# The second score product of prompt attention: over all 128 rows with a zero-padded low part of the query, and the odd heads' value rows kept in the tile of the norm factors

## The chip, the cores and the metric

One core of one Trainium2 chip runs the kernel. The metric is device microseconds (us) of one execution; the kernel before was timed three times (2570.28, 2571.55 and 2572.80 us, median 2571.55 us). The engines are named as in the profile: PE is the matrix engine, and PEld its weight loads, DVE the vector engine, ACT the scalar engine, POOL the general engine, and SP the queue that issues most of the DMAs.

## The reference, cut to what matters

The kernel does one inference step of a two-layer decoder trunk for a prompt of 1024 tokens and for 8 x 8 sampled tokens. The change lies in the stick-breaking attention of layer 0 over the prompt: 8 heads of 64, strictly causal, no softmax. For each head and each block of 128 queries:

```python
z = jnp.einsum('nqhd,nkhd->nhqk', qblk, k, preferred_element_type=jnp.float32) * scale + bias_f
mask = k_pos[None, :] < pblk[:, None]
log_1m = jnp.where(mask, jax.nn.log_sigmoid(-z), 0.0)
after = lax.cumsum(log_1m, axis=3, reverse=True) - log_1m
logw = jnp.where(mask, jax.nn.log_sigmoid(z) + after, -jnp.inf)
wgt = jnp.exp(logw)
return jnp.einsum('nqhk,nkhd->nqhd', wgt.astype(v.dtype), v)
```

## The kernel before

All large products are made from operands split in two: a high part, rounded to the matrix engine's reduced float32 format, and the low part that is left (the line L235, `mm3`, makes three matmuls of each product in this way). PE is fed by one stream of matmuls in program order. The prompt is worked on in two halves of the tokens: group A holds the tokens 0 to 511, group B the rest with the 64 sampled tokens. The attention isn't a stage of its own. It is a generator, and the loops of the large products (the input projection of group B, the output projection and the channel mixer of group A) call it at fixed places: each call puts a piece of attention between two stretches of L235 matmuls. So the order of the work on each engine is fixed by the program; nothing is moved at run time. In the profile the attention of group A runs from about 228 to 335 us beside the input projection of B, and that of group B from about 344 to 565 us beside the output projection and the channel mixer of A.

The function `attention` handles 32 units in each group: 8 heads, and for each of them four blocks of 128 queries, the longest key range first (512, 384, 256 and 128 keys in A; 1024, 896, 768 and 640 in B).

- `operands` (L951 to L963) prepares a head. Two heads share a 128-partition tile, the even one in the partitions 0 to 63, the odd one in 64 to 127. Call the head's own half r and the other one o. The tile `kt` holds the high part of the keys in r (ACT) and the low part in o (DVE); `qa` holds the high part of the queries in both halves (ACT). `qz` is one tile for all heads: its half r gets the low part of the queries (DVE, L963).
- `s1` (L971 to L988) makes the scores. One matmul over 128 rows takes `qa` and `kt`, so both the high and the low part of the keys with the high part of the queries; a second one over 64 rows takes the half r of `qz` and of `kt`, and adds the low part of the queries. Both are on L981. Ranges over 512 keys are cut in two column blocks, so group B has four such matmuls in a unit and group A has two (of at least 256 columns). ACT makes two sigmoids out of the scores (L986), POOL sets one column (L988).
- `s2`, one unit later, is on DVE: two scans (L995, L998) and one product (L1000) that makes the weights in `be`.
- `s3`, again one unit later, transposes the weights on PE (L1010) and copies them by ACT (L1011). It stands just ahead of the scores of the unit after next.
- `s4`, on every second unit, multiplies the transposed weights with the value rows `vrow` (L1020). `load_v` (L965) fetches the value rows of a head by a DMA from SP's queue; `vrow` had two buffers that the heads take in turn.

The tile `rr` (128 partitions x 1088 columns) holds the factor of the current norm, spread over all partitions, for both groups: columns 0 to 511 for A, 512 to 1087 for B. L284 writes it, L291, L908 and L924 read it.

Of the kernel before, what the change touches and what calls it, by code (L numbers as in the profile page):

```python
# [8 lines left out]
F = mybir.dt.float32  # L9
FR = mybir.dt.float32r  # L10
I32 = mybir.dt.int32
AF = mybir.ActivationFunctionType
OP = mybir.AluOpType
# [16 lines left out]
def f32(ap):  # L30
    return ap.bitcast(F)
# [13 lines left out]
HALF = 512  # L45
GA = Grp(0, HALF, (0, 1, 512, 0))
GB = Grp(HALF, T, (0, 2, 288, 0))
# [10 lines left out]
def trunk_kernel(ctx, tc, x_prompt, x_sample, cache_k, cache_v, state_conformer, state_shortconv, state_pool,  # L58
# [4 lines left out]
    pe, act, dve, pool, sp = nc.tensor, nc.scalar, nc.vector, nc.gpsimd, nc.sync  # L63
# [28 lines left out]
    rr = consts.tile([128, T], F, name="rr")  # L92
# [129 lines left out]
    def w_next(live=0):  # L222
        j = wj[0]
        wj[0] += 1
        w_split(j + 3 - live)
        w_load(need(j + 6 - live))
        return hls.pop(j)
# [411 lines left out]
    def ms():  # L639
        return mp.tile([128, 512], F, name="m")  # L640
# [296 lines left out]
    def attention(g):  # L937
        i0, i1 = g.t0, g.t0 + 4
        NKEY = 128 * i1
        units = [(h, i) for h in range(8) for i in range(i1 - 1, i0 - 1, -1)]  # L940
        with ExitStack() as es_:
            pa = es_.enter_context(tc.tile_pool(name=f"pa{g.c0}", bufs=1))
            zp = es_.enter_context(tc.tile_pool(name=f"zp{g.c0}", bufs=1, space=PSUM, side="right"))
            op_ = es_.enter_context(tc.tile_pool(name=f"op{g.c0}", bufs=1, space=PSUM, side="right"))

            qz = pa.tile([128, HALF], FR, name="qz")
            kt_, qa, vrow, small = {}, {}, {}, []

            def operands(h):  # L951
                hp, hh = divmod(h, 2)
                r, o = slice(hh * 64, hh * 64 + 64), slice(64 - hh * 64, 128 - hh * 64)
                k = kt_[h] = pa.tile([128, NKEY], FR, name="kt", bufs=2)
                q = qa[h] = pa.tile([128, HALF], FR, name="qa", bufs=2)
                ks, qs = kall[r, hp, 0:NKEY], qall[r, hp, g.c0:g.c0 + HALF]
                small.append(lambda: act.activation(k[r], ks, AF.Copy))
                small.append(lambda: act.activation(q[r], qs, AF.Copy))
                for c in range(0, NKEY, 512):
                    small.append(lambda c=c: dve.tensor_tensor(k[o, c:c + 512], ks[:, c:c + 512],  # L960
                                                               f32(k[r, c:c + 512]), op=OP.subtract))
                small.append(lambda: act.activation(q[o], qs, AF.Copy))
                small.append(lambda: dve.tensor_tensor(qz[r], qs, f32(q[r]), op=OP.subtract))  # L963

            def load_v(h):  # L965
                vrow[h] = pa.tile([128, i1, 64], F, name="vrow", bufs=2)
                sp.dma_start(vrow[h], v_p[0, 0].rearrange("(t p) h d -> p t h d", p=128)[:, 0:i1, h])

            bt, qt, wt = {}, {}, {}

            def s1(u):  # L971
                h, i = units[u]
                n = 128 * (i + 1)
                nb = 1 if n <= 512 else 2
                w = n // nb
                nm = max(w, 256)
                z = zp.tile([128, 1 if g is GA else 2, 512], F, name="z2")
                for b in range(nb):
                    r = slice(h % 2 * 64, h % 2 * 64 + 64)
                    for s, (q, k) in enumerate(((qa[h], kt_[h]), (qz[r], kt_[h][r]))):  # L980
                        pe.matmul(z[:, b, :nm], q[:, (i - i0) * 128:(i - i0) * 128 + 128], k[:, b * w:b * w + nm],  # L981
                                  start=s == 0, stop=s == 1)
                q = qt[u] = pa.tile([128, NKEY], F, name="q2", bufs=2)
                be = bt[u] = pa.tile([128, NKEY], F, name="be", bufs=2)
                for o, sgn, bi in ((q, -0.125, 1), (be, 0.125, 0)):
                    act.activation(o[:, :n].rearrange("p (b w) -> p b w", b=nb), z[:, 0:nb, :w], AF.Sigmoid,  # L986
                                   scale=sgn, bias=bh[:, bi, h:h + 1])
                pool.memset(be[:, n - 1:n], 0.0)  # L988

            def s2(u):  # L990
                n = 128 * (units[u][1] + 1)
                be, q = bt[u], qt.pop(u)

                e = q[:, n - 128:n][:, ::-1]
                dve.tensor_tensor_scan(e, e, ident[:, ::-1], 0.0, op0=OP.mult, op1=OP.max)  # L995
                if n > 128:
                    e = q[:, 0:n - 128][:, ::-1]
                    dve.tensor_tensor_scan(e, e, ones[:, 0:1].to_broadcast([128, n - 128]), q[:, n - 128:n - 127],  # L998
                                           op0=OP.mult, op1=OP.mult)
                dve.tensor_tensor(be[:, 0:n - 1], be[:, 0:n - 1], q[:, 1:n], op=OP.mult)  # L1000

            def s3(u):
                i = units[u][1]
                be = bt.pop(u)
                w = wt[u] = pa.tile([128, i1 - u % 2, 128], F, name=f"wt{u % 2}")
                for j0 in range(0, i + 1, 4):
                    n = min(4, i + 1 - j0)
                    m = ms().rearrange("p (j n) -> p j n", j=4)
                    for j in range(n):
                        pe.transpose(m[:, j], be[:, (j0 + j) * 128:(j0 + j) * 128 + 128], ident)  # L1010
                    act.activation(w[:, j0:j0 + n], m[:, :n], AF.Copy)  # L1011

            def s4(u):
                h, i = units[u]
                hp, hh = divmod(h, 2)
                ws = wt.pop(u - 1), wt.pop(u)
                o = op_.tile([128, 128], F, name="o2")
                for j in range(i + 2):
                    for b in range(2 if j <= i else 1):
                        pe.matmul(o[64 * b:64 * b + 64], vrow[h][:, j], ws[b][:, j], start=j == 0, stop=j == i + 1 - b)  # L1020
                for b in range(2):
                    c = (i + 1 - b) * 128
                    act.activation(qall[hh * 64:hh * 64 + 64, hp, c:c + 128], o[64 * b:64 * b + 64], AF.Copy)

            load_v(0)
            operands(0)
            while small:
                small.pop(0)()
            for _ in range(3):
                yield 1  # L1030
            for u in range(len(units) + 3):
                if u >= 3 and u % 2 == 0:
                    s4(u - 3)
                if 2 <= u < len(units) + 2:
                    s3(u - 2)
                if 1 <= u < len(units) + 1:
                    s2(u - 1)
                if g is GB:
                    yield 1
                if u < len(units):  # L1040
                    h, r = divmod(u, 4)
                    if r == 0 and h < 7:
                        operands(h + 1)
                    if r == 2 and h < 7:
                        load_v(h + 1)
                    s1(u)
                for _ in range(2):
                    if small:
                        small.pop(0)()
                yield 1  # L1050
# [263 lines left out]
    def flow_ab():  # L1314
        while "start" not in phase:
            yield None
        with tc.tile_pool(name="conv", bufs=1) as ep, \
                tc.tile_pool(name="cacc", bufs=1, space=PSUM, side="right") as cp:
            yield from conv_a(ep, cp)
        yield from conv_norm(GA)  # L1320
        while "B" not in phase:
            yield None
        yield from attention(GA)
# [38 lines left out]
    def flow_c():  # L1362
        yield from attention(GB)
        kstack.close()
        with tc.tile_pool(name="convb", bufs=1) as ep, \
                tc.tile_pool(name="caccb", bufs=1, space=PSUM, side="right") as cp:
            conv, attn = conv_b(ep, cp), sample()
            some, wait = True, False
            while some:
                some = False  # L1370
                piece = next(attn, 0)
                if piece != 1:
                    wait = not wait
                    if wait or not piece:
                        some = next(conv, 0) != 0
                some = some or piece != 0
                yield 1
        yield from conv_norm(GB)
# [346 lines left out]
    for n in range(2, KC):  # L1725
        h = w_next()
# [5 lines left out]
    with tc.tile_pool(name="fab", bufs=1) as ep:  # L1732
        gen = forms_a(ep)
        for n in range(KC):
            h = w_next()
# [257 lines left out]
```

## Time and profile before

| what | value |
| --- | --- |
| median of the three runs | 2571.55 us |
| the profiled execution's own time | 2568.46 us |
| its span | 2566.7 us |
| granted clock of PE, mean | 0.991 |
| busy share of the span: PE, PEld, DVE, ACT, POOL | 96%, 86%, 66%, 43%, 61% |
| matmuls of L981, first and second product | 96 and 96 |
| median duration of one, first (128 rows) and second (64 rows) | 393 ns, 442 ns |
| matmuls with the value rows (L1020), all groups | 576 |
| share of the chain that ended last: PE, DVE | 45%, 8% |

In the rows of the profile, a matmul is written with the rows and columns of its weights and the shape of what streams through: "64\*128 64x512" is a product over 64 rows with 512 columns. A duration is the whole passage of one matmul through the engine, and matmuls overlap; what one of them costs is the time from its start to the start of the next one. "issue" marks idle time for which the profile shows no event that was waited for. The number in square brackets is the idle time of the engine just ahead of the row.

### The profile page before, as it was taken

The numbers are of one execution on the slowest core, as the hardware profiler recorded it, in microseconds if no ns is written. First come the engines' busy times: TensorE is split into PE (matmuls) and PEld (weight loads), VectorE is DVE, ScalarE is ACT, GpSimd is POOL, SyncE is SP. The second block draws the span as 40 slices with busy tenths as digits, with TensorE's granted clock in tenths as the row PEclk, the third lists the DMA queues.
The fourth block names the chain that finished last, engine by engine and source line by source line (L and its number), as shares of the span: only waits on it lengthen the run. The fifth ranks groups of instructions, "written<-read, shape, count | busy, mean of one in ns | idle before, by whom it ended". The sixth has DMA issues, their size and how long they took to land.

```text
span 2566.7 us, 41423 instructions
## 1 busy us (share of the span) xinstructions
PE 2467.6 (96%) x15871; PEld 2196.0 (86%) x15871; DVE 1695.6 (66%) x2359; ACT 1106.1 (43%) x1875; POOL 1562.3 (61%) x1201
## 2 busy tenths in 40 slices
PE   8999999999999989999999999999999999999998
PEld 6788876777777768989999889989888888999997
DVE  3696767867878844567656633348777778666655
ACT  4536766754444334334333521234433444443333
POOL 6754234434443346678777722266888886887775
PEclk9999999999999999999999999999999999999999
DMA  7342231225455534222323411152323332333322
GB/s 220 114 113 74 65 105 50 62 66 158 143 171 166 148 108 156 70 74 83 99 83 99 129 42 42 44 158 61 92 85 97 99 99 83 107 95 103 99 84 79
DMA packets 355485, 258.31 MB, mean 101 GB/s; under 512 B 22913, under 2 KB 303617, under 8 KB 355272
## 3 DMA queue, kind: packets, MB, share of 16 engines
q1 hardware_dynamic: 355256, 255.66, 33.9%
q8 instruction: 126, 2.06, 0.3%
q14 instruction: 71, 0.58, 0.1%
q10 hardware_dynamic: 32, 0.01, 0.0%
HBM read 237.41 MB, written 18.69 MB: 100 GB/s over the span
## 4 chain that ended last, share of the span: by engine, by line
PE 45%; DVE 8%; POOL 2%; issue 1%; ACT 1%; POOLq 0%; DVEq 0%; ACTq 0%
PE acc L235 24%; PE acc L521 20%; POOL hl L197 1%; DVE hid L241 1%; DVE sum L200 1%; DVE sum L201 1%; DVE hb L295 1%; DVE b L1673 0%; DVE tmp L525 0%; DVE sum_c L214 0%; DVE sum L202 0%; DVE fb L1677 0%; PE blk L1896 0%; DVE x L1673 0%; POOL tmp L500 0%
## 5 line engine op out<-in xcount | busy, mean ns | idle before, releaser
L186 POOL TENSOR_TENSOR hl<-stage,hl 128x512 fp32r<-128x512 f32 x464 | 638.1, 1399 | 461.1 <-ACT hl L184 336.4
L235 PE MATMUL acc<-x,hl 128*128 128x512 f32 (+1 forms) x3648 | 788.4, 354 | 12.6 <-DVE hb L295 2.6
L235 PEld LDWEIGHTS acc<-x,hl 128*128 128x128 f32 x3648 | 584.8, 191 | 84.6 <-issue 14.1
L235 PE MATMUL acc<-hid,hl 128*128 128x288 f32 (+1 forms) x3096 | 551.3, 334 | 18.5 <-DVE hb L295 8.9
L235 PEld LDWEIGHTS acc<-hid,hl 128*128 128x128 f32 x3096 | 471.5, 190 | 72.4 <-DVE hb L295 13.0
L295 DVE TENSOR_TENSOR hb<-acc,hb 128x512 f32<-128x512 f32 (+1 forms) x360 | 256.1, 718 | 177.2 <-PE acc L235 175.8
L521 PE MATMUL acc<-x,hl 128*128 128x288 f32 (+1 forms) x2676 | 362.8, 291 | 4.7 <-POOL hl L197 1.9
L521 PEld LDWEIGHTS acc<-x,hl 128*128 128x128 f32 x2676 | 349.4, 189 | 7.1 <-POOL hl L197 2.7
L184 ACT ACTIVATE hl<-stage 128x1024 fp32r<-128x1024 f32 x232 | 243.6, 1055 | 224.0 <-PE acc L235 139.9
L197 POOL TENSOR_TENSOR hl<-sum,hl 128x512 fp32r<-128x512 f32 x180 | 237.1, 1345 | 168.5 <-ACT hl L196 168.5
L525 DVE TENSOR_TENSOR tmp<-acc,tmp 128x288 f32<-128x288 f32 (+1 forms) x420 | 173.5, 441 | 228.2 <-ACT tmp L537 135.4
L197 POOL TENSOR_TENSOR hl<-stage,hl 128x512 fp32r<-128x512 f32 x180 | 267.1, 1505 | 13.3 <-ACT hl L196 13.3
L521 PE MATMUL acc<-b,hl 128*128 128x256 f32 (+1 forms) x1548 | 216.6, 291 | 13.2 <-DVE tmp L525 10.3
L521 PEld LDWEIGHTS acc<-b,hl 128*128 128x128 f32 x1548 | 202.3, 190 | 18.8 <-ACT hl L196 8.5
L235 PE MATMUL acc<-x1t,hl 128*128 128x288 f32 x1152 | 216.4, 296 | 1.5 <-POOL hl L186 1.5
L235 PEld LDWEIGHTS acc<-x1t,hl 128*128 128x128 f32 x1152 | 196.1, 189 | 19.4 <-POOL hl L186 1.7
L196 ACT ACTIVATE hl<-sum 128x512 fp32r<-128x512 f32 x180 | 103.1, 623 | 237.2 <-DVE sum L202 212.3
L291 DVE TENSOR_TENSOR tmp<-acc,rr 128x512 f32<-128x512 f32 (+1 forms) x108 | 75.1, 709 | 111.1 <-PE acc L235 99.1
L500 POOL TENSOR_TENSOR tmp<-tmp 128x576 f32<-128x576 f32 (+1 forms) x85 | 127.6, 1501 | 16.3 <-ACT tmp L477 8.3
L196 ACT ACTIVATE hl<-stage 128x512 fp32r<-128x512 f32 x180 | 105.6, 618 | 67.3 <-PE acc L235 62.0
L241 DVE TENSOR_TENSOR hid<-tmp,hid 128x512 fp32r<-128x512 f32 (+1 forms) x88 | 100.0, 1138 | 48.1 <-ACT hid L240 47.8
L235 PE MATMUL acc<-x1a,hl 128*128 128x512 f32 x480 | 122.4, 409 | 3.0 <-POOL hl L186 1.3
(287 smaller groups left out, 3162.4 us busy)
## 6 DMA issues: line engine op xcount, KB each, us to landing
stage<-in_w_ffn_in_dram SPq DMA_DIRECT2D x176, 512.0 KB
stage<-in_w_ffn_out_dram SPq DMA_DIRECT2D x88, 512.0 KB
stage<-in_w_in_even_dram SPq DMA_DIRECT2D x40, 512.0 KB
kst<-in_cache_k_dram SPq DMA_DIRECT2D x64, 256.0 KB
vst<-in_cache_v_dram SPq DMA_DIRECT2D x64, 256.0 KB
stage<-in_w_out_even_dram SPq DMA_DIRECT2D x16, 512.0 KB
stage<-in_w_in_odd_dram SPq DMA_DIRECT2D x16, 512.0 KB
stage<-in_w_out_odd_dram SPq DMA_DIRECT2D x16, 512.0 KB
```

The lines of the kernel that those rows point to most:

```text
L184: act.activation(hl[:, 0], st, AF.Copy)
L186: pool.tensor_tensor(hl[:, 1, c], st[:, c], f32(hl[:, 0, c]), op=OP.subtract)
L196: act.activation(hl[:, 0, c], x, AF.Copy)
L197: pool.tensor_tensor(hl[:, 1, c], x, f32(hl[:, 0, c]), op=OP.subtract)
L200: todo = [lambda: dve.tensor_tensor(sb, su[:, lo], su[:, hi], op=OP.add), lambda: dve.tensor_tensor(sa[:, hi], sg[:, lo], su[:, lo], op=OP ...
L235: pe.matmul(acc[:, b, :c1 - c0], w, xs[:, xi, c0 - o:c1 - o], start=first and s == 0, stop=last and s == 2)
L241: (on or dve).tensor_tensor(dst[:, 1], src, f32(dst[:, 0]), op=OP.subtract)
L291: dve.tensor_tensor(d, a, r, op=OP.mult)
L295: dve.tensor_tensor(d, a, d, op=OP.add)
L500: (dve if both and f == NF - 1 else pool).tensor_tensor(t[:, :n], t[:, :n], u[:, :n], op=OP.mult)
L521: pe.matmul(acc[:, :w2], h[:, wi, i, k], xk[:, xi], start=k == 0 and s == 0, stop=k == 3 and s == 2)
L525: dve.tensor_tensor(out, acc[:, :w2], x, op=OP.add)
```

## The change

The second product no longer takes 64 rows of `qz` and `kt` but all 128 of both. For that there are now two tiles `qz`, one for even and one for odd heads; each is set to zero in its half o once per group (POOL, L948), and its half r gets the low part of the queries as before. The zeros meet the low part of the keys, so the second product's value is what it was. The number of matmuls and of streamed columns is the same.

The second `qz` takes 2 KB of each partition. In group B the buffer for the odd heads' value rows is given up for it: their 8 x 64 values per partition are now loaded into the columns 512 to 1023 of `rr`. The even heads, and all heads of group A, keep a tile of their own.

```diff
-            qz = pa.tile([128, HALF], FR, name="qz")
+            qz = [pa.tile([128, HALF], FR, name=f"qz{i}") for i in range(2)]
+            for i in range(2):
+                pool.memset(f32(qz[i][64 - 64 * i:128 - 64 * i]), 0.0)
...
-                small.append(lambda: dve.tensor_tensor(qz[r], qs, f32(q[r]), op=OP.subtract))
+                small.append(lambda: dve.tensor_tensor(qz[hh][r], qs, f32(q[r]), op=OP.subtract))
...
-                vrow[h] = pa.tile([128, i1, 64], F, name="vrow", bufs=2)
+                if h % 2 and g is GB:
+                    vrow[h] = rr[:, HALF:2 * HALF].rearrange("p (t d) -> p t d", t=i1)
+                else:
+                    vrow[h] = pa.tile([128, i1, 64], F, name=f"vrow{h % 2}")
...
                 for b in range(nb):
-                    r = slice(h % 2 * 64, h % 2 * 64 + 64)
-                    for s, (q, k) in enumerate(((qa[h], kt_[h]), (qz[r], kt_[h][r]))):
-                        pe.matmul(z[:, b, :nm], q[:, (i - i0) * 128:(i - i0) * 128 + 128], k[:, b * w:b * w + nm],
+                    for s, q in enumerate((qa[h], qz[h % 2])):
+                        pe.matmul(z[:, b, :nm], q[:, (i - i0) * 128:(i - i0) * 128 + 128], kt_[h][:, b * w:b * w + nm],
                                   start=s == 0, stop=s == 1)
```

From L946 on, the lines of the new kernel stand 2 to 5 further down (L981 is now L985, L1000 is L1004, L1010 is L1014).

The order of the instructions changes on POOL alone, by two fills in each group. These are POOL's rows where the attention of group B begins, in the kernel before; "waits" names the engines and DMA lanes whose semaphores an instruction waits for.

```order
L988 MEMSET be 128x1 [waits DVE_49,PE_49,Activation_49]
L186 TENSOR_TENSOR hl<-stage,hl 128x512 [waits DMAHW2_49,PE_49,Activation_49]
L186 TENSOR_TENSOR hl<-stage,hl 128x512
L988 MEMSET be 128x1 [waits DMAHW0_49,DMAHW1_49,DVE_49,DMAHW3_49,PE_49,DMAHW5_49,Activation_49,Pool_49]
L988 MEMSET be 128x1 [waits Activation_49]
L186 TENSOR_TENSOR hl<-stage,hl 128x512 [waits DMAHW6_49,Activation_49]
```

And the same place in the changed kernel:

```order
L992 MEMSET be 128x1 [waits DVE_49,PE_49,Activation_49]
L186 TENSOR_TENSOR hl<-stage,hl 128x512 [waits DMAHW2_49,PE_49,Activation_49]
L186 TENSOR_TENSOR hl<-stage,hl 128x512
L948 MEMSET qz_3505 64x512 [waits DMAHW1_49,DMAHW0_49,DMAHW3_49,DVE_49,DMAHW5_49,PE_49,Pool_49]
L948 MEMSET qz_3506 64x512
L992 MEMSET be 128x1 [waits Activation_49,Pool_49]
L992 MEMSET be 128x1 [waits Activation_49]
L186 TENSOR_TENSOR hl<-stage,hl 128x512 [waits DMAHW6_49,Activation_49]
```

The two fills stand ahead of the first column fill of the unit, and have taken over its wait for the memory of the stage before. What is queued behind them are the column fills and the weight split (L186) of the large products.

On PE the same matmuls stand in the same order. These are the first scores of group B before (z is the score tile):

```order
L981 MATMUL z_3539<-kt,qa 128x512 [waits DVE_49,Activation_49]
L981 MATMUL z_3539<-kt,qz 128x512 [waits DVE_49]
L981 MATMUL z_3539<-kt,qa 128x512
L981 MATMUL z_3539<-kt,qz 128x512
L235 MATMUL acc<-x_5_76,hl 128x512 x6
```

And in the changed kernel:

```order
L985 MATMUL z_3545<-kt,qa 128x512 [waits DVE_49,Activation_49]
L985 MATMUL z_3545<-kt,qz_3505 128x512 [waits DVE_49,Pool_49]
L985 MATMUL z_3545<-kt,qa 128x512
L985 MATMUL z_3545<-kt,qz_3505 128x512
L235 MATMUL acc<-x_5_76,hl 128x512 x6
```

Only the wait for POOL's fill is new, once in each group. On DVE, ACT and SP nothing changes its place; on SP the DMAs of the odd heads' value rows name `rr` as their target, and their waits are those that they had.

## The prediction

> **What bounds the kernel now.** I read the page first: the span, the busy shares, and the chain that ended last.
>
> ```profile
> span 2566.7 us, 41423 instructions
> PE 2467.6 (96%) x15871; PEld 2196.0 (86%) x15871; DVE 1695.6 (66%) x2359; ACT 1106.1 (43%) x1875; POOL 1562.3 (61%) x1201
> PE 45%; DVE 8%; POOL 2%; issue 1%; ACT 1%; POOLq 0%; DVEq 0%; ACTq 0%
> ```
>
> PE is the engine whose program sets the time: it is busy for 96%, and the chain is mostly PE's. A matmul that is saved shortens the run as far as the others keep pace. So I asked for the busy times in the two stretches with prompt attention (PE, PEld, DVE, ACT, POOL, then the granted clock), and one right behind them.
>
> ```profile
> 225.00:345.00 120.00, 115.99 (x787) 96.67 (x786) 87.34 (x126) 87.72 (x191) 30.86 (x53) 0.97 0.26 71
> 345.00:560.00 215.00, 207.52 (x1171) 149.02 (x1170) 169.96 (x161) 143.45 (x222) 89.66 (x85) 0.98 0.23 65
> 560.00:580.00 20.00, 20.00 (x111) 16.00 (x108) 6.82 (x9) 8.48 (x18) 12.15 (x11) 1.00 0.45 124
> ```
>
> PE leads in both stretches, but DVE follows: 170 of 215 us in the second. Then I asked who waited for whom from 225 to 560 us (total, times, longest).
>
> ```profile
> DVE q L995 <- ACT q L986: 30.4, 19, 3.3
> PEld z L981 <- issue: 26.3, 111, 0.4
> PEld acc L235 <- issue: 9.9, 47, 0.4
> PE m L1010 <- DVE be L1000: 3.2, 3, 2.7
> ```
>
> The weight loads of L981, and those of L235 that mostly follow one, stand idle for 36.2 us with nothing to wait for that the profile shows. PE's real waits for DVE are few so far. DVE itself waits for the sigmoids, that is, for PE's scores one step earlier. What the idle loads mean shows in order of time: PE's rows around a unit of group B with 768 keys (start, duration).
>
> ```profile
> 478.89 0.34 PE L981 MATMUL z<-kt,qa 128*128 128x384 f32 x1
> 479.15 0.44 PE L981 MATMUL z<-kt,qz 64*128 64x384 f32 x1
> 479.52 0.44 PE L981 MATMUL z<-kt,qa 128*128 128x384 f32 x1
> 479.89 0.44 PE L981 MATMUL z<-kt,qz 64*128 64x384 f32 x1
> 480.26 1.68 PE L235 MATMUL acc<-x,hl 128*128 128x512 f32 x6
> 481.78 0.93 PE L1010 MATMUL m<-ident,be 128*128 128x128 f32 x7
> ```
>
> The attention of the sampled tokens has a group of the same size, four score matmuls with 384 columns, but all over 128 rows, and six L235 matmuls behind it:
>
> ```profile
> 592.55 0.87 PE L1140 MATMUL z<-kth,qb 128*128 128x384 f32 x4
> 593.27 1.56 PE L235 MATMUL acc<-hid,hl 128*128 128x512 f32 x6
> 594.67 0.60 PE L1117 MATMUL m<-ident,kst 128*128 128x128 f32 x4
> ```
>
> From the first score to what follows the six, the first group takes 481.78 - 478.89 = 2.89 us, the second one 594.67 - 592.55 = 2.12 us. The work is equal; the difference is that the first group changes between 128 and 64 rows four times. That makes 0.77 us, or 0.19 us for each change of the row count.
>
> **The change part by part.** *The second product over 128 rows.* In group B, 32 units lose four changes each: 32 x 0.77 = 24.6 us. In group A a unit has one score pair, so two changes. Its rows, two long runs of L235 for the price of a matmul without any change, and six L235 right behind short transposes:
>
> ```profile
> 256.81 0.48 PE L981 MATMUL z<-kt,qa 128*128 128x512 f32 x1
> 257.22 0.50 PE L981 MATMUL z<-kt,qz 64*128 64x512 f32 x1
> 257.66 1.86 PE L235 MATMUL acc<-x,hl 128*128 128x288 f32 x12
> 259.36 0.27 PE L1010 MATMUL m<-ident,be 128*128 128x128 f32 x1
> ...
> 568.75 11.52 PE L235 MATMUL acc<-x,hl 128*128 128x512 f32 x48
> 580.11 0.49 PE L1117 MATMUL m<-ident,kst 128*128 128x128 f32 x3
> ...
> 1009.76 50.43 PE L235 MATMUL acc<-x,hl 128*128 128x288 f32 x377
> ...
> 482.46 1.65 PE L235 MATMUL acc<-x,hl 128*128 128x512 f32 x6
> 483.95 0.31 PE L981 MATMUL z<-kt,qa 128*128 128x320 f32 x1
> ```
>
> A 512-column matmul costs (580.11 - 568.75)/48 = 0.237 us and a 288-column one 50.43/377 = 0.134 us. The pair and the twelve behind it take 259.36 - 256.81 = 2.55 us; without changes that would be 2 x 0.237 + 12 x 0.134 = 2.08 us, and behind short transposes a weight load is exposed anyhow: the six at 482.46 take 1.49 us in place of 6 x 0.237 = 1.42, so 0.07 us. That leaves 0.40 us for a unit, 12.8 us for 32. PE's program shrinks by 24.6 + 12.8 = 37.4 us. The idle loads above give nearly the same (36.2 us) by another way.
>
> The Trainium skill gives a price for a matmul that can't overlap its neighbour (TensorE: Matmul & The Clock Gate, "Single matmul latency" and "Back-to-back issue gap"): about (398 + N)/2.4 ns alone against N/2.4 + 2.5 ns in a stream, so 163 ns more. By that estimate 192 changes would be 31.4 us; the rows, which have the duration here, say 37.4, and I take these.
>
> *What DVE gives back.* The transposes of a unit need its weights from DVE. Three units' ends of L1000 on DVE, and the start of their transposes on PE (in A, in A, in B):
>
> ```profile
> 239.11 0.56 DVE L1000 TENSOR_TENSOR be<-be,q 128x383 f32<-128x383 f32 x1
> 239.72 0.55 PE L1010 MATMUL m<-ident,be 128*128 128x128 f32 x3
> 264.00 1.54 DVE L1000 TENSOR_TENSOR be<-be,q 128x383 f32<-128x383 f32 x1
> 265.59 0.55 PE L1010 MATMUL m<-ident,be 128*128 128x128 f32 x3 [0.22 <-DVE be L1000]
> 503.42 2.07 DVE L1000 TENSOR_TENSOR be<-be,q 128x895 f32<-128x895 f32 x1
> 505.63 0.95 PE L1010 MATMUL m<-ident,be 128*128 128x128 f32 x7
> ```
>
> PE starts 0.05, 0.05 and 0.14 us after DVE's end: there, time saved on PE turns into waiting. I went through the 64 units in this way; twelve, six in each group, stand under 0.6 us, the others mostly between 1 and 3 us. How much such a unit gives back: DVE's chain starts from the unit's own scores, or from those of the unit before when DVE has not caught up. PE saves, between those scores and the transposes, half a pair's worth (0.2) plus one or two whole units: 0.6 to 1.0 us in A, 0.97 to 1.74 us in B. Less the small margins I take 0.7 us for A, and for B 1.5, near the upper end, since its longer scans make DVE lag behind for more than a unit. 6 x 0.7 + 6 x 1.5 = 13.2 us given back. The bounds: nothing, if DVE's own queue tightens as well, and twice as many units, 26.4 us, if the next tight ones join. Less than nothing I exclude: DVE's work for a unit is unchanged, and its start can only come earlier.
>
> *POOL's fills.* Four fills of 64x512. The trace has one such:
>
> ```profile
> L1080 POOL MEMSET vnew<- x1: 522/522/522, 574.3 to 574.3; 64x512 f32 x1
> 343.87 2.54 POOL L186 TENSOR_TENSOR hl<-stage,hl 128x512 fp32r<-128x512 f32 x2 [11.79 <-ACT hl L184]
> 352.64 0.10 POOL L988 MEMSET be<- 128x1 f32 x1 [6.22 <-issue]
> 349.02 0.50 PE L981 MATMUL z<-kt,qz 64*128 64x512 f32 x1
> ```
>
> In group B, POOL is free from 346.41 us, and the first product that needs the zeros starts at 349.02. Two fills end at 346.41 + 2 x 0.52 = 347.45: covered, with 1.6 us to spare, if the memory that they write is free by then. The wait for that memory stood at the column fill, at 352.64; so it was over by then, and the worst that it can cost is 352.64 + 0.52 - 349.02 = 4.1 us, once. Nothing speaks for that end, since the stage before has finished with its last transposes well ahead; I take 0. In group A POOL is idle for three quarters of the stretch (30.9 of 120 us busy): 0. Without that cover the four fills would be 2.1 us.
>
> *Value rows in `rr`.* The same DMAs at the same places on SP, with unchanged waits; the two halves of `rr` belong to the two groups, and group B's factors have been read for the last time before:
>
> ```profile
> 336.48 0.76 DVE L291 TENSOR_TENSOR tmp<-acc,rr 128x576 f32<-128x576 f32 x1 [4.28 <-PE acc L235]
> ```
>
> The first odd head's load stands after group B's first units, behind 349 us. Cost 0; the bounds are one load's delay either way, and no engine waits for these loads in the waits above.
>
> *Sum.* 37.4 - 13.2 = 24.2 us. On the profiled execution's time, 2568.46 us, that gives 2544.3 us; this execution is 3.1 us below the median of the runs shown, 2571.55 us, from which I get 2547.3 us. About 0.2%, or 5.1 us, is what a measurement can tell from no change.
>
> **The rivals.**
>
> 1. *DVE takes over in group B.* After the change PE has 215 - 24.6 = 190.4 us for the second stretch, and DVE 170 us of work in it, 89%. If twice as many units wait, 26.4 us come back: 2571.55 - 37.4 + 26.4 = 2560.6 us. For it: DVE's 30.4 us of waiting for sigmoids show that its idle time doesn't lie where it would be needed. Against it: most units have over 1 us in hand.
>
> 2. *All of it is kept.* The engines shift together, and the twelve units give nothing back: 2534.2 us. Against it: the wait of 0.22 us in the row at 265.59 shows that some units are at their limit now.
>
> 3. *No gain, because the row count isn't the cause.* If a weight load can't start while a matmul over the same rows is in flight, the pair costs as much at 128 rows, and the time stays 2571.6 us. This is a rule of the Trainium skill (TensorE: Matmul & The Clock Gate, part 3, "The mechanism"): weight loads overlap with matmuls in flight only when their row groups differ. The trace doesn't bear it out: the 48 L235 matmuls behind 568.75 us each have a weight load for the same 128 rows, and follow each other every 0.237 us, and the four of L1140 need 0.72 us together.
>
> 4. *Slower: the clock.* The stretches with attention have a granted clock of 0.97 and 0.98 against 1.00 behind them. If fuller products pull it down further, PE's 323.5 us there grow by 3.3 us for each hundredth. The gain is used up at 7.3 hundredths, and from 8.9 (a clock of 0.89) on the kernel is slower by over 0.2%; at 0.88 (9.5 hundredths, 31.4 us) it would be 2571.55 - 24.2 + 31.4 = 2578.8 us. Against it: the 20 us behind 560 us are filled with PE work without a 64-row product, and run at 1.00.
>
> **How the numbers follow.** Forecast (some 18 to 30 us gained): 0.74. Rival 1: 0.13; rival 2: 0.06; rival 3: 0.04; rival 4: 0.03. Faster by over 0.2%: 0.74 + 0.13 + 0.06 = 0.93; within 0.2%: 0.04; slower: 0.03. The predicted time is the forecast's, 2547.3 us. The range goes from rival 2's end, 2534 us, to rival 1's, 2561 us, which are also the bounds of what DVE gives back; it leaves out rivals 3 and 4 and the far side of rival 1.
>
> **What would show it right or wrong.** In the profile after, the second product must read 128\*128, its pitch must be that of L235 (0.237 us at 512 columns in place of 0.43), and the issue idle ahead of the scores (26.3 us) must nearly vanish, with PE's busy time some 37 us lower. PE's waits for `be` must grow from 3.2 us to some 13 us; if they stay small, rival 2 was right, and at 25 us or over, rival 1. Behind 565 us everything must run as before, only earlier. The forecast is wrong if the pitch of the pair stays (rival 3), if the clock of the two stretches falls below 0.95 (rival 4), or if the first scores of group B wait for POOL.

## The result and the profile after

| | before | after |
| --- | --- | --- |
| median of 4 runs each | 2570.91 us (2566.35 to 2572.80) | 2550.07 us (2549.11 to 2553.31) |
| ratio, 95% interval | | 0.9922 [0.9909, 0.9936] |
| profiled execution, its span | 2568.46, 2566.7 us | 2549.70, 2547.9 us |

The kernel is 20.8 us faster; the forecast was 24.2 us. The page of the kernel after:

```profile
span 2547.9 us, 41426 instructions
PE 2434.8 (96%) x15871; PEld 2194.1 (86%) x15871; DVE 1701.0 (67%) x2359; ACT 1104.0 (43%) x1875; POOL 1566.5 (61%) x1205
PE 43%; DVE 9%; POOL 3%; issue 2%; ACT 1%; POOLq 0%; DVEq 0%; ACTq 0%
```

The number of matmuls is the same, 15871, and PE is busy for 32.8 us less (2467.6 before). The chain that ended last gives PE two points less and DVE one more: the other engines begin to show. The busy times of the kernel after in the two stretches with prompt attention and in one right behind (PE, PEld, DVE, ACT, POOL, granted clock):

```profile
225.00:336.00 111.00, 104.01 (x795) 94.92 (x794) 89.20 (x126) 86.48 (x191) 32.40 (x56) 0.98 0.28 78
336.00:537.00 201.00, 184.27 (x1165) 149.41 (x1163) 172.92 (x161) 142.75 (x222) 93.78 (x87) 0.97 0.25 69
537.00:557.00 20.00, 19.98 (x107) 15.88 (x107) 6.84 (x9) 8.48 (x18) 12.26 (x11) 1.00 0.43 122
```

The first stretch is 9 us shorter, the second 14 us. In the second one DVE now has 172.9 us of work in 201, and PE stands idle for 16.7 us, against 7.5 us before. What it waits for shows in the waits of the kernel after from 225 to 560 us (total, times, longest):

```profile
DVE q L999 <- ACT q L990: 18.3, 17, 2.3
PE m L1014 <- DVE be L1004: 12.2, 11, 3.5
PEld m L1014 <- ACT qa L964: 6.2, 3, 2.4
PEld m L1014 <- DVE be L1004: 4.9, 6, 1.0
```

The transposes (L1014, before L1010) now wait 12.2 us for `be` as against 3.2. The rows of PEld are idle time of the weight loads, in which PE may still be busy with the matmul before. The idle time without a cause ahead of the scores has left the list; that ahead of the value products and the transposes stays (9.1 and 7.6 us, before 8.7 and 7.0). For the score line itself (L985), all instructions of the second product in the kernel after (ns min/median/max), and the idle time put down to issue:

```profile
L985 PE MATMUL z<-kt,qz x96: 278/338/763, 231.3 to 533.5; 128*128 128x512 f32 x24, 128*128 128x384 f32 x24, 128*128 128x256 f32 x16, 128*128 128x448 f32 x16
  issue: 0.6, 2
```

It reads 128\*128, its median is 338 ns in place of 442, and the 26.3 us of issue idle in 111 pieces are 0.6 us in 2. In order of time, rows of the kernel after around a unit of A with 512 keys, then the first second product of group B with what comes ahead of it, then around a unit of B with 768 keys (start, duration; idle time ahead in brackets):

```profile
255.19 0.48 PE L985 MATMUL z<-kt,qa 128*128 128x512 f32 x1
255.50 0.39 PE L985 MATMUL z<-kt,qz 128*128 128x512 f32 x1
255.73 1.76 PE L235 MATMUL acc<-x,hl 128*128 128x288 f32 x12
257.33 0.27 PE L1014 MATMUL m<-ident,be 128*128 128x128 f32 x1
...
337.33 1.09 POOL L948 MEMSET qz<- 64x512 f32 x2
338.45 0.68 DVE L965 TENSOR_TENSOR qz<-hb,qa 64x512 fp32r<-64x512 f32 x1
339.28 0.47 PE L985 MATMUL z<-kt,qz 128*128 128x512 f32 x1 [0.85 <-DVE qz L965]
...
462.87 0.34 PE L985 MATMUL z<-kt,qa 128*128 128x384 f32 x1
463.05 0.33 PE L985 MATMUL z<-kt,qz 128*128 128x384 f32 x1
463.22 0.34 PE L985 MATMUL z<-kt,qa 128*128 128x384 f32 x1
463.39 0.34 PE L985 MATMUL z<-kt,qz 128*128 128x384 f32 x1
463.57 1.57 PE L235 MATMUL acc<-x,hl 128*128 128x512 f32 x6
464.98 0.93 PE L1014 MATMUL m<-ident,be 128*128 128x128 f32 x7
```

The unit of B takes 464.98 - 462.87 = 2.11 us, before 2.89, and the four products follow each other every 0.17 us, before 0.26 and 0.37. The unit of A takes 2.14 us, before 2.55; the second product at 255.50 holds PE for 0.23 us, before 0.44. At the start of B, PE waits 0.85 us for the low part of the queries. DVE starts to write it 0.03 us after POOL's two fills end, but it was busy with its subtraction before (L962) until 338.41 us, so the fills did not hold it up; and in the kernel before without its second scan (below), which has no fills, PE waits 0.75 us at the same place. The profile puts 1.13 us of idle time of the weight load there down to POOL, but the fills had ended 0.83 us before that load started; DVE's subtraction ended last.

For the comparisons below, every trace has the same 15871 weight loads of PE, so the same load marks the same place in the program. Column A is the time from load 1000 to load 1900 (the attention of A and what stands beside it), B from 1900 to 3200, "later" from 10600 to 12700, a stretch of the second half without prompt attention. All in us of one profiled execution each.

| kernel | A | B | later | span |
| --- | --- | --- | --- | --- |
| before | 131.40 | 240.78 | 322.02 | 2566.7 |
| before, a second execution | 131.43 | 239.42 | 324.32 | 2566.0 |
| after | 122.02 | 226.82 | 325.63 | 2547.9 |
| after, a second execution | 122.07 | 226.83 | 325.20 | 2546.6 |
| after, 64 rows again (e_rows64) | 131.39 | 240.78 | 322.45 | 2567.1 |
| 128 rows in A only (e_onlyA) | 122.05 | 239.41 | 326.50 | 2559.3 |
| 128 rows in B only (e_onlyB) | 131.43 | 229.13 | 324.00 | 2558.0 |
| before, fewer changes in B (e_order64) | 131.41 | 230.98 | 327.34 | 2564.2 |
| before without the second scan (e_noscan_before) | 130.33 | 230.22 | 324.23 | 2555.9 |
| after without the second scan (e_noscan_after) | 117.98 | 208.04 | 324.76 | 2525.7 |
| after, transposes later in B (e_late) | 121.99 | 223.60 | 322.61 | 2544.3 |
| after, low keys on POOL in B (e_pool_kt) | 122.27 | 236.07 | 322.65 | 2553.3 |
| both of these (e_late_pool_kt) | 122.05 | 228.09 | 321.66 | 2549.8 |

### The profile page after: what moved, and what is told of

Its sections match the earlier page's. It is cut to its first block, busy times and chain, and to the rows that moved or that the text cites. A ratio compares the mean times of both kernels' runs of the same rounds, so it can differ in the third digit from the quotient of the medians.

```text
span 2547.9 us, 41426 instructions
## 1 busy us (share of the span) xinstructions
PE 2434.8 (96%) x15871; PEld 2194.1 (86%) x15871; DVE 1701.0 (67%) x2359; ACT 1104.0 (43%) x1875; POOL 1566.5 (61%) x1205
## 4 chain that ended last, share of the span: by engine, by line
PE 43%; DVE 9%; POOL 3%; issue 2%; ACT 1%; POOLq 0%; DVEq 0%; ACTq 0%
PE acc L235 22%; PE acc L521 19%; DVE sum L200 2%; POOL hl L197 2%; DVE hid L241 1%; DVE hb L295 1%; DVE sum L201 1%; DVE sum L202 1%; DVE tmp L525 0%; DVE b L1677 0%; POOL tmp L500 0%; DVE sum_c L214 0%; DVE fb L1681 0%; DVE x L1677 0%; PE blk L1900 0%
## 5 line engine op out<-in xcount | busy, mean ns | idle before, releaser
L186 POOL TENSOR_TENSOR hl<-stage,hl 128x512 fp32r<-128x512 f32 x464 | 639.5, 1402 | 456.1 <-ACT hl L184 334.9
L235 PE MATMUL acc<-x,hl 128*128 128x512 f32 (+1 forms) x3648 | 781.7, 352 | 13.6 <-ACT hl L184 3.3
L235 PEld LDWEIGHTS acc<-x,hl 128*128 128x128 f32 x3648 | 587.5, 190 | 76.2 <-issue 4.9
L235 PE MATMUL acc<-hid,hl 128*128 128x288 f32 (+1 forms) x3096 | 553.7, 334 | 19.0 <-DVE hb L295 8.8
L235 PEld LDWEIGHTS acc<-hid,hl 128*128 128x128 f32 x3096 | 472.1, 190 | 74.6 <-DVE hb L295 12.6
L521 PE MATMUL acc<-b,hl 128*128 128x256 f32 (+1 forms) x1548 | 216.5, 291 | 14.9 <-DVE tmp L525 11.9
L235 PE MATMUL acc<-x1t,hl 128*128 128x288 f32 x1152 | 216.3, 296 | 1.5 <-POOL hl L186 1.5
L235 PEld LDWEIGHTS acc<-x1t,hl 128*128 128x128 f32 x1152 | 195.9, 188 | 19.5 <-POOL hl L186 1.7
L235 PE MATMUL acc<-x1a,hl 128*128 128x512 f32 x480 | 122.4, 408 | 3.0 <-POOL hl L186 1.3
```

The source lines that it names most:

```text
L186: pool.tensor_tensor(hl[:, 1, c], st[:, c], f32(hl[:, 0, c]), op=OP.subtract)
L235: pe.matmul(acc[:, b, :c1 - c0], w, xs[:, xi, c0 - o:c1 - o], start=first and s == 0, stop=last and s == 2)
L521: pe.matmul(acc[:, :w2], h[:, wi, i, k], xk[:, xi], start=k == 0 and s == 0, stop=k == 3 and s == 2)
```

## The experiments

The theory: PE pays for each change between 128-row and 64-row products, the change removes 192 of them, and DVE, which can't follow everywhere, takes about a third back. The rivals: it is something else in the edit (the two tiles, the fills, the value rows in `rr`); DVE takes nothing back and the price is smaller; what is missing is lost elsewhere.

**The rows alone put back.** The kernel after, with its two tiles, fills and `rr`, but the second product over 64 rows:

```diff
-                    for s, q in enumerate((qa[h], qz[h % 2])):
...
+                    r = slice(0, 128) if False else slice(h % 2 * 64, h % 2 * 64 + 64)
+                    for s, (q, k) in enumerate(((qa[h], kt_[h]), (qz[h % 2][r], kt_[h][r]))):
...
```

> The changed kernel with its two padded tiles, its fills and the value rows in rr, but the second product over 64 rows again. Theory (each change between 128 and 64 rows costs PE 0.19 us): the gain is gone, about 2571 us, between 2566 and 2575. Rival (the gain comes from the second tile, the fills or the moved value rows): it stays near 2550 us.

Measured: 2572.03 us against 2572.04 of the kernel before, ratio 0.9995 [0.9986, 1.0004]. The line's instructions and idle time in this kernel:

```profile
L986 PE MATMUL z<-kt,qz x96: 379/442/792, 229.6 to 555.1; 64*128 64x512 f32 x24, 64*128 64x384 f32 x24, 64*128 64x256 f32 x16, 64*128 64x448 f32 x16
  issue: 26.3, 111
```

The idle time is back to the tenth of a microsecond, 111 pieces of it, and A and B of the table are those of before. So the whole gain comes from the row count, and the rest of the edit costs nothing that shows.

**One group at a time.** The same edit as above with the 64 rows left in one of the groups (the line for A; for B it reads `g is GB`):

```diff
...
+                    r = slice(0, 128) if g is GA else slice(h % 2 * 64, h % 2 * 64 + 64)
...
```

> The changed kernel with the second product over 128 rows in group A alone, over 64 in group B. Theory: 64 changes of the row count are gone, 12.8 us of PE time less about 4 us given back to waits for DVE: 2562 us, 2559 to 2565. Rival (the change in group B alone matters, since only its units have two blocks): about 2571 us.

> The changed kernel with the second product over 128 rows in group B alone. Theory: 128 changes are gone, 24.6 us of PE time, of which waits for DVE take 10 to 12: 2558 us, 2555 to 2561. Rival (nothing is given back in B): 2546 us.

Measured: 128 rows in A alone 2563.78 us, 0.9963 [0.9950, 0.9977], 8.3 us faster; in B alone 2557.46 us, 0.9932 [0.9918, 0.9946], 14.6 us faster. The two add up to 22.9 us, about what the full change gives, and the table places each gain in its own column. B alone is 2.3 us longer than in the full change (229.13 against 226.82), so the part of the gain in B that depends on what went before is small. PE is idle for as long in both (18.4 us of B); what differs is the granted clock, 0.96 against 0.98.

**Fewer changes with the 64 rows kept.** In the kernel before, both column blocks of the first product, then both of the second, so that a unit of B changes its row count twice and not four times; in A there is one block and nothing moves:

```diff
-                for b in range(nb):
-                    r = slice(h % 2 * 64, h % 2 * 64 + 64)
-                    for s, (q, k) in enumerate(((qa[h], kt_[h]), (qz[r], kt_[h][r]))):
+                r = slice(h % 2 * 64, h % 2 * 64 + 64)
+                for s, (q, k) in enumerate(((qa[h], kt_[h]), (qz[r], kt_[h][r]))):
+                    for b in range(nb):
```

> The kernel before, its second product over 64 rows, but in group B both blocks of the first product come first and then both blocks of the second, so that a unit has two changes of the row count in place of four. Theory (the price is one of the change): 64 changes fewer, 12.4 us of PE time, and after what DVE takes back 6 to 10 us: 2561 to 2565 us. Rival (the price belongs to each product over 64 rows, whatever stands beside it): no change, 2571 us.

Measured: 2561.03 us, 0.9950 [0.9937, 0.9964], 11.0 us faster, B shorter by 9.8 us. The unit with 768 keys in this kernel:

```profile
473.94 0.51 PE L981 MATMUL z<-kt,qa 128*128 128x384 f32 x2
474.38 0.62 PE L981 MATMUL z<-kt,qz 64*128 64x384 f32 x2
474.93 1.67 PE L235 MATMUL acc<-x,hl 128*128 128x512 f32 x6
```

and the idle time of its score line:

```profile
  issue: 12.4, 47
```

The four products take 474.93 - 473.94 = 0.99 us; in the order of before it was 1.37 us, over 128 rows 0.70 us. The idle pieces fall from 111 to 47, by exactly the 64 changes that are gone, and each took 13.9/64 = 0.22 us with it. So it is the change of the row count that costs, not a product over 64 rows in itself. This agrees with the Trainium skill (TensorEngine Tiling (Array Packing), "Key Properties"), which says that the engine is drained when its tiling mode is switched; the page has no price, and the rows here say 0.19 to 0.22 us. A drain as such is not seen in any row.

**How much DVE takes back.** Both kernels without the second scan, one of DVE's three steps for a unit, so that DVE is early and PE nearly alone sets the pace:

```diff
-                    dve.tensor_tensor_scan(e, e, ones[:, 0:1].to_broadcast([128, n - 128]), q[:, n - 128:n - 127],
-                                           op0=OP.mult, op1=OP.mult)
+                    pass
```

> The kernel before without the longer of the two scans (L998), so that DVE has some 90 us less to do in the attention; the weights are not the reference's. Its time alone says little: theory and rival both expect a few us under 2571, since PE's waits for DVE there are 3 to 5 us. It is the yardstick for the next run.

> The changed kernel without the longer scan, again with weights that are not the reference's. Theory (what is missing from 37.4 us is given back in waits for DVE): it is 33 to 38 us faster than the kernel before without that scan. Rival (the saving on PE is only some 21 to 24 us, and DVE takes nothing): 20 to 24 us.

Measured: 2557.69 us (0.9956 [0.9939, 0.9974]) and 2526.31 us (0.9828 [0.9809, 0.9847]); between them 31.4 us, where the two full kernels differ by 20.8. That is short of the expected 33 to 38, and far from the rival's 20 to 24. The two stretches of the pair, before and then after, both without the scan:

```profile
225.00:341.00 116.00, 112.58 (x781) 94.55 (x780) 65.28 (x99) 84.79 (x186) 29.01 (x52) 0.99 0.24 67
341.00:552.00 211.00, 209.00 (x1195) 150.72 (x1194) 103.49 (x136) 149.40 (x233) 80.10 (x87) 1.00 0.25 70
```

```profile
225.00:329.00 104.00, 99.69 (x783) 91.17 (x782) 67.47 (x100) 83.25 (x187) 30.10 (x55) 1.00 0.27 75
329.00:518.00 189.00, 185.87 (x1196) 152.92 (x1195) 107.67 (x136) 148.18 (x233) 80.91 (x89) 0.99 0.27 78
```

PE is busy for 98% of these stretches in the first kernel and 97% in the second, and for 112.58 + 209.00 - 99.69 - 185.87 = 36.0 us less in the second. By the table A gains 12.35 and B 22.18 us, 34.5 us together; the other 3 us to 31.4 lie in the stretch from load 3200 to load 10600, which has no prompt attention and took 3.3 us longer in the second trace. The full kernels keep 9.4 in A and 13.3 in B (means of the two executions each), 22.6 us. So 11.9 us are taken back by DVE's pace, 3.0 in A and 8.9 in B.

Taken unit by unit, from a unit's first score to the end of the L235 stretch behind it, this pair shows the price at every width: 29 of the 32 units of A save 0.38 to 0.42 us, and 29 of the 32 of B 0.77 to 0.80. Nearly all of the 2.4 us that B falls short of 24.6 lies behind one unit of 896 keys, in a long stretch of L235 matmuls. Two rows of the kernel before there, then two of the kernel after and its granted clock, all without the scan:

```profile
427.79 0.74 PE L235 MATMUL acc<-x,hl 128*128 128x512 f32 x2 [0.28 <-ACT hl L184]
429.22 6.12 PE L235 MATMUL acc<-x,hl 128*128 128x512 f32 x25 [0.70 <-POOL hl L186]
```

```profile
405.96 0.73 PE L235 MATMUL acc<-x,hl 128*128 128x512 f32 x2 [1.26 <-ACT hl L184]
407.39 7.61 PE L235 MATMUL acc<-x,hl 128*128 128x512 f32 x25 [0.70 <-POOL hl L186]
407.34:410.75 3.41, 3.36 (x8) 2.69 (x9) 3.04 (x4) 2.21 (x4) 3.41 (x3) 0.50 0.13 39
```

PE, now earlier, waits 1.26 us in place of 0.28 for the high part of a weight that ACT makes (1.25 in the full kernel after), and here the next 25 matmuls take 1.5 us longer, 3.41 us of them at a granted clock of 0.50.

What I had not expected is how much the scan's removal gains in the kernel before: 10.8 us, though PE waited only 3.2 us for `be` there. DVE's `x` (L382) is a second wait of PE for a late DVE, 2.6 us, which is gone too; the last section comes back to the rest.

**Both kernels once more.** A repeat of the kernel after with the pair above, and one of the kernel before later.

> The changed kernel once more, for a second trace. Theory (the 4 us lost between 1800 and 2230 us of the first trace are scatter of the later stages): about 2550 us, and the second trace loses them elsewhere or not at all. Rival (the earlier start shifts the later stages against each other for good): the same 4 us at the same places.

> The kernel before once more, for a second trace. Theory (how long the stretch from 1793 to 2115 us of the trace of before takes belongs to each kernel, since two traces of the changed kernel agree in it): 322 us again from PE's weight load 10600 to 12700. Rival (scatter of single executions): anything from 322 to 327 us.

Measured: the kernel after 2546.51 us, 0.9903 [0.9883, 0.9923], 22.0 us faster; the kernel before, timed once, 2567.75 us. The traces of after agree to 0.05 us in A and 0.01 us in B, those of before to 0.03 and 1.4 us. The "later" stretch is 325.6 and 325.2 us after and 322.0 and 324.3 us before. So 0.9 to 3.6 us of the gain seem to be lost there; but kernels that differ only in group A or B spread there from 321.7 to 327.3 us, and no rule showed. This is what the second expectation calls scatter of single executions, and not its 322 us; it stays open what makes it.

**The transposes later.** In the kernel after, `s3` in group B stands one call later, behind the L235 stretch in place of ahead of it, which gives DVE the time of six matmuls more:

```diff
-                if 2 <= u < len(units) + 2:
+                if g is GA and 2 <= u < len(units) + 2:
                     s3(u - 2)
...
                     yield 1
+                    if 2 <= u < len(units) + 2:
+                        s3(u - 2)
```

> The changed kernel with the transposes of group B moved behind the stretch of large products that follows them, so that DVE has about 1.5 us more for each unit's weights. Theory (waits for those weights take 11 to 12 us in group B): most of them go, 6 to 10 us gained on the changed kernel: 2540 to 2544 us. Rival (the wait moves on to the copies, the value products or the scores): about 2550 us.

Measured: 2542.59 us, 0.9894 [0.9877, 0.9910]; on the same chip 3.9 us less than the kernel after, short of the expected 6 to 10 and with intervals that overlap. B is 3.2 us shorter. One wait of this kernel from 337 to 537 us, and its last 105 us of group B:

```profile
PE m L1014 <- DVE be L1004: 7.6, 7, 2.4
```

```profile
432.00:537.00 105.00, 99.39 (x668) 80.99 (x665) 100.90 (x88) 78.70 (x125) 54.42 (x48) 1.00 0.21 61
```

The waits for `be` fall only from 9.0 us (337 to 541 us of the kernel after) to 7.6 us, and DVE is now busy for 100.9 of 105 us (96.5 in the last 105 us of B in the kernel after). More time ahead of the transposes helps little once the engine that makes the weights is full: this points to DVE's work, not its position, as the bound in this part. A part of that work is new: for the same 174 instructions of B DVE is busy for 188.8 us here, 182.8 in the kernel after.

**Work taken off DVE.** The low parts of the keys (L962), 13.1 us of DVE's work in B, on POOL; alone, and with the transposes later.

```diff
-                    small.append(lambda c=c: dve.tensor_tensor(k[o, c:c + 512], ks[:, c:c + 512],
+                    small.append(lambda c=c: (pool if g is GB else dve).tensor_tensor(k[o, c:c + 512], ks[:, c:c + 512],
```

> The changed kernel with the low part of the keys made by POOL in place of DVE in group B, 16 subtractions of 64x512 less for DVE, some 13 us. Theory (in group B the changed kernel is bound by DVE's total work): 5 to 9 us faster than the changed kernel, 2538 to 2545 us. Rival (it is bound by single late products, or POOL's additional work stretches DVE's as much as it takes from it): 2547 to 2552 us or slower.

> Both edits, the later transposes and the low keys on POOL in group B. Theory (DVE's total work is the bound, and the later transposes only let it be used fully): 6 to 10 us faster than with the later transposes alone, 2533 to 2538 us. Rival (the two edits take away the same waits): no more than 2 us better than the better one of them.

Measured: 2554.64 us, 0.9936 [0.9921, 0.9952], and 2548.29 us, 0.9912 [0.9895, 0.9928]. Neither is an improvement, against the expectation of both, and B alone is 9.2 us longer by the first, 4.5 us by the second than without it. Groups of instructions in group B, with the work on DVE (the kernel after) and then on POOL (the first of the two kernels; busy us and mean ns, then idle before):

```profile
L1002 DVE TENSOR_TENSOR_SCAN q<-q,ones 128x896 f32<-128x896 f32 (+3 forms) x32 | 61.1, 1909 | 1.1
L962 DVE TENSOR_TENSOR kt<-kall,kt 64x512 fp32r<-64x512 f32 x16 | 13.1, 859 | 1.9 <-ACT kt L959 1.7
```

```profile
L235 PEld LDWEIGHTS acc<-x,hl 128*128 128x128 f32 x389 | 73.9, 197 | 21.0 <-POOL hl L186 5.0 <-ACT hl L184 1.7
L1002 DVE TENSOR_TENSOR_SCAN q<-q,ones 128x896 f32<-128x896 f32 (+3 forms) x31 | 64.9, 2094 | 1.1
L962 POOL TENSOR_TENSOR kt<-kall,kt 64x512 fp32r<-64x512 f32 x16 | 27.6, 1743 | 0.6
```

The subtraction takes POOL 1743 ns in the mean, DVE 859 ns. DVE's scans grow beside it, from 1909 to 2068 ns over all 32 (the row above leaves one short scan out), and the weight loads of L235 stand idle for 5.0 us because POOL's low operand parts (L186) come late. All of B, from load 1900 to load 3200, in the kernel after and then with the keys on POOL (PE, PEld, DVE, ACT, POOL, granted clock):

```profile
325.01:551.83 226.82, 208.46 (x1302) 168.86 (x1301) 182.76 (x174) 157.17 (x253) 103.95 (x96) 0.98 0.26 74
```

```profile
325.20:561.27 236.07, 213.92 (x1303) 172.90 (x1301) 182.89 (x158) 157.07 (x253) 128.80 (x112) 0.95 0.25 71
```

DVE has 16 instructions less and is busy for as long as before: all that was taken off it came back in longer instructions, as the rival of the first run says. Of the 9.2 us, 3.8 are idle time of PE, and 5.5 are the same PE work taking longer at the lower granted clock, 0.95. Since no time of DVE was freed, the two runs don't try the theory that DVE's total work is the bound. The limit of DVE in B is shown by the runs without the scan, and this remedy isn't one.

## Why the prediction held, point by point

- **What bounds the kernel: right.** PE's busy time fell by 32.8 us (forecast some 37) and the span by 18.8 us; where the other engines keep pace (the pair without the scan), 36.0 us less of PE's busy time made 34.5 us less of time.
- **The price of a change, 0.19 us: right.** A unit of B was forecast at 2.12 us and takes 2.11; for one of A the forecast was 0.40 us, the rows quoted show 0.41. The sum of 37.4 us was 3 us high against the pair's 34.5: 12.35 us in A (forecast 12.8) and 22.18 in B (24.6). The price isn't what was off: the units of B save 0.77 to 0.80 us at every width, those of A 0.38 to 0.42, but for three in each group. What the sum did not have is that PE, being early, waits elsewhere too: in B 1.0 us more for ACT ahead of one long L235 stretch, and 1.5 us at the lower clock behind it. The estimate of 31.4 us from the Trainium skill was the lower one: 163 ns for a change, where the units show about 0.20 us.
- **Given back at DVE, 13.2 us: right in kind; the size came out closer than its working.** 11.9 us by the runs; 3.0 in A (forecast 4.2) and 8.9 in B (9.0). The wait that was named reached 12.2 us for "some 13", but that is a rise of 9.0 us; most of the rest is PE waiting for POOL's column fill and for the low queries at the start of B, 0.85 us more each. Nor are the units quite those that were counted: in the trace of before ten stand under 0.6 us, five in each group, not twelve. In A the five did become the ones that wait, 0.5 us more each. In B one of the five waits no longer than before, and 2.2 of the 6.4 us more come from two units that had 1.7 and 2.3 us in hand. So the 9.0 us for B is in part luck. Its bounds hold: neither rival 1 (26.4 us) nor rival 2 (none) came.
- **Fills: cost right, margin wrong.** The pair of fills took 1.09 us, forecast 1.04. The 1.6 us to spare were computed on the times of before; in fact POOL came to the fills only at 337.33 and ended them at 338.42, 0.03 us ahead of DVE's subtraction into the same tile, and PE, now earlier, waited 0.85 us for that subtraction. The place where I had looked for cover had moved with the change. The wait that the profile puts down to POOL there, which the prediction named as a sign against it, ended with DVE's subtraction. The run with 64 rows shows no cost.
- **Value rows in `rr`: right**, by the same run.
- **No gain (rival 3): wrong**, and with it, for this stream, the rule of the Trainium skill that it cited. Loads for the same 128 rows do overlap here: the products of the 768-key unit follow every 0.17 us although a weight load stands before each.
- **Slower by the clock (rival 4): did not come.** The granted clock of the two stretches went from 0.97 and 0.98 to 0.98 and 0.97. The last section shows what it falls behind.
- **The net, 24.2 us: 2 to 3 us high.** 20.8 and 22.0 us were measured. A and B give 22.6 us of it; the forecast gross is 2.9 us high and what DVE takes back 1.3 us high, which make up the difference of 1.6 us between 24.2 and 22.6. The rest would be the "later" stretch, which the forecast took to run as before, and where it is not settled that anything is lost.

## What to carry to other kernels

A matmul over fewer rows is not a cheaper one when it stands singly among matmuls over all rows: count the changes of the row count, not the rows, and if the free rows can be filled with zeros, or the same kind put next to each other, each change avoided gives about 0.2 us of PE. Then read, unit by unit, how long before its use the next engine's result is ready: the part of PE's gain that exceeds that margin turns into waiting, here a third. Where the waiting begins, moving the consumer later helps little if the producer is full (3.9 us here, within the noise), and a shift of work to an engine that is slower at it can cost more than it frees: here the 13 us that were moved freed none of DVE's time.

## What the runs showed of the hardware that was not expected

**A wait can cost clock besides its own time.** The granted clock is the third column from the end of a row. In these traces it is 1.00 or 0.50, and it changes only at the borders of pieces of 3.41 us; the values between come from stretches that hold both. Two pairs of such pieces in the kernel before, with the two long waits of its group B (for `be`, then for `x` of L382):

```profile
360.66:364.08 3.42, 0.85 (x4) 0.35 (x2) 3.28 (x3) 2.17 (x3) 3.42 (x2) 1.00 0.73 201
364.08:367.49 3.41, 3.32 (x12) 2.96 (x13) 3.35 (x3) 1.09 (x2) 2.80 (x3) 0.50 0.44 109
439.17:442.58 3.41, 1.26 (x5) 1.05 (x6) 3.02 (x4) 2.21 (x3) 2.84 (x2) 1.00 0.56 156
442.58:445.99 3.41, 3.41 (x11) 2.50 (x10) 0.38 (x1) 0.31 (x1) 0.00 (x0) 0.50 0.40 117
```

and the second of these waits in the second execution of the same kernel:

```profile
439.01:442.42 3.41, 1.80 (x7) 1.19 (x8) 2.86 (x3) 2.52 (x3) 2.27 (x2) 1.00 0.57 168
442.42:445.83 3.41, 3.41 (x19) 2.93 (x20) 0.87 (x6) 0.26 (x1) 0.00 (x0) 1.00 0.20 59
```

The wait for `x` is 2.6 us both times. In the first execution PE is busy for 1.26 us of the piece that holds most of it, and the next piece runs at 0.50; in the second one the wait lies across a border, PE is busy for 1.80 us, and the clock stays at 1.00; B is 1.4 us shorter there. All thirteen traces, cut at these borders from 200 to 600 us, say the same: behind each of the 44 pieces with PE busy for less than 48% the clock was 0.50; from 49 to 53% it was so behind 9 of 19; of 1462 busier pieces only three were followed by one at 0.50, and these ran at 0.50 themselves. So the idle time comes first and the lower clock behind it. It is read from traces; no run set the waits by itself.

This accounts for the scan. All of B in the kernel before, with the scan and without it:

```profile
334.17:574.95 240.78, 231.69 (x1303) 168.37 (x1301) 179.90 (x174) 157.72 (x253) 99.68 (x94) 0.98 0.25 70
```

```profile
333.25:563.48 230.23, 226.61 (x1303) 164.98 (x1302) 107.93 (x142) 157.62 (x253) 86.85 (x94) 1.00 0.26 73
```

PE is idle for 5.5 us less and busy for 5.1 us less, with three pieces at 0.50 in the first row and none in the second. But a wait does not always cost this: the kernel after is idle for 18.4 us of B, twice as long as the kernel before, and has three such pieces too.

The Trainium skill (TensorE: Matmul & The Clock Gate, Part 1, "What's actually happening") says that the throttled state is the default and activity releases it, with idle time bringing it back; the trace agrees, and here a piece in which PE is idle for some half of the time is enough. So rival 4 had the wrong cause: no fuller product lowered the clock.

**An engine beside another.** Moving 13.1 us of work from DVE to POOL took nothing off DVE's busy time in B (182.76 us in the kernel after, 182.89 with the keys on POOL), since DVE's instructions become longer beside POOL's. With the keys on POOL, four of the eight scans of 640 columns in B run while POOL does no tensor operation, and take 1.55 us each; the other four have POOL working beside them and take 2.38 to 2.41 us.
